# Retention's queries and keys with the head's values on partitions, rope in that layout

## The chip, the cores and the metric

The kernel runs on one core of a Trainium2 chip. The engines of that core are TensorE (PE: matmuls; PEld is its loading of weights, which the profile lists apart), VectorE (DVE), ScalarE (ACT), GpSimd (POOL) and SyncE (SP, which here only issues DMA transfers). On-chip memory has 128 partitions; PE leaves its results in PSUM, in banks of 128 x 512 values.

The metric is device time in microseconds (us), the median over runs. A profiled execution gives the trace from which the rows come. Its span runs from the first to the last instruction.

## The reference

The program is a trunk of two layers over one sequence of 256 tokens with 2048 values each, all in float32. Each layer normalises x, applies a gain and a shift that come from `c` (adaLN), makes one wide projection, feeds three branches (retention, a gated linear recurrence, latent attention), merges them by gates, projects once more and adds the result to x. Retention has 8 heads of 128 values. What bears on the change:

```python
def apply_rope(x, cos, sin):
    half = x.shape[-1] // 2
    x1, x2 = x[..., :half], x[..., half:]
    return concatenate([x1 * cos - x2 * sin, x2 * cos + x1 * sin], axis=-1)

# rope_tables: ang[token, i] = positions[token] * 10000 ** (-2 i / dim), i < dim / 2
cos_ret, sin_ret = rope_tables(positions, 128)     # retention: 64 frequencies
cos_mla, sin_mla = rope_tables(positions, 64)      # latent attention: 32 frequencies

# for each layer
h = rms_norm(x, norm_pre) * (1 + scale) + shift    # scale, shift: from c @ ada_w
rq, rk, rv, rg, lx, lg, mq, mkv, mkr, mg, merge_logits = split(h @ w_in)
q = apply_rope(rq as [256, 8, 128], cos_ret, sin_ret) * 128 ** -0.5
k = apply_rope(rk as [256, 8, 128], cos_ret, sin_ret)
scores = einsum('bnihd,bnjhd->bhnij', q, k) * intra_decay    # and a state between chunks of 64
```

## The kernel before

**Products.** Every weight is split into a head of 12 bits (`wh`, a cast by ACT, L291) and the exact rest (`wl`, a subtraction by DVE, L292), and the activations likewise. A product is then three matmuls, head by head, head by rest, rest by head. Weights come by SP's queue as tiles `raw` of 128 x 2048 values, 1 MB each, in the order in which they are used: one tile is two d-tiles (2 x 128 rows of the weight) by 1024 columns.

Two helpers do the products of 1024 columns over 16 d-tiles. `gemm_x` (matmul on L349) holds the activations still and streams the weights: tokens end on partitions, 128 of them in each half `hf`, and a d-tile takes 12 matmuls of 512 columns. In the last tile of a product the first half of the tokens ends ahead of the second. `gemm_w` (L367 to L369) holds the weights still, in 8 blocks of 128 columns, and streams the 256 tokens: the columns end on partitions, and a d-tile takes 24 matmuls of 256 columns. Both fill four PSUM banks out of six (`acc`); two more (`mi`) are for small work. `group` empties the four, each with one ACT instruction (L396, L398), into two slots of 128 x 1024; where a product of layer 0 is made in parts, DVE adds up the parts (L394). `mode_of` says which helper does which product: `lx`, `lg` and `mg` use `gemm_w`, all others `gemm_x`.

**Order.** The kernel is written as a main run of large products with chains of small work beside them. `tick` is called after each weight tile; it goes through the chains that are ready and lets each do a step. Each engine then runs its own instructions in that order. DMA issues stand on SP's queue (weights, x) and on POOL's (small loads).

In each layer the order is `lx`, `lg`, `mqkv`, `mg`, the gates of `lru`, `mkr`, `rq`, then the two `lru` branch products (`branch`), `rk`, the up-projections of latent attention, `rv`, `rg`, and so on. In the trace, layer 0's `rq` lies around 360 to 408 us, its two `lru` branches at 408 to 455, its `rk` at 506 to 550. In layer 0 the adaLN sums of layer 1 run beside all of that: `ada_sum` lets DVE multiply and add rows of `ada_w` (L452, L454), with a share for ACT (L445) and POOL (L449). In layer 1 no such sums run.

**Retention's queries and keys.** `rq` and `rk` come out of `gemm_x` with tokens on partitions. `ret_chain` waits for `rq`, calls `ret_rope`, which calls `rope` (L592 to L595) four times: two products of 128 x 256 with the sine, one of 128 x 512 with the cosine and one addition of 128 x 512 each, all on DVE. The scores want the head's 128 values on partitions, so `ret_turn` turns the result: four groups for each operand, each of four PE transposes (L771) into one bank `mi`, which ACT copies out (L772), one group for a step of the chain. Then the same for `rk`. Two operands in each of two layers are 16 groups.

**The start.** The first instructions load x, `c`, the vectors and the positions (`pos_i`, L187, on POOL's queue), cast the positions (L189), work out the softplus of `lru_lambda` (from L242 on) and the sums of squares of x (`xtot`, L533), whose square root (L406) gives the norm of x. The rope tables are made later, in the chain `tables`: `k_freq` is loaded onto all partitions (L193, issued at 40.95 us), and 16 operations on DVE make angles, fold them into range and clamp them, each over [128 tokens, 2 halves, 96 frequencies], 64 for retention and 32 for latent attention. Eight ACT instructions take the sines, into `cosr`, `sinr` (retention) and `cosm`, `sinm` (latent attention), all with tokens on partitions.

## Time and profile before

| | before |
|---|---|
| runs, us | 2019.4, 2019.5, 2023.18 |
| median, us | 2019.5 |
| span of the profiled execution, us | 2016.0 |
| instructions in the trace | 25350 |
| DMA, MB moved | 456.98 |
| mean DMA rate over the span, GB/s | 227 |
| granted PE clock, mean over the span (1 is full speed) | 0.991 |

The profiled execution has no time of its own beside its span; the median of the runs is 3.5 us above it, for what lies around the first and the last instruction.

The profile's rows are read like this. An engine's busy time is a sum over instructions. PE's instructions are pipelined, so the duration of one matmul is longer than its share of the time: the distance between starts is what counts. The chain that ended last is followed back from the last instruction to what released each step, and its shares by engine add up to the span. A list of waits says which engine stood idle, for whom, how long in all, how often, and the longest. A timeline has one instruction, or a run of equal ones, in a row: start, duration, engine, line, operation, result and operands, shape; in brackets the idle time ahead of it and what ended it.

### The profile page before, as it was taken

What the parts mean: (1) busy time and instruction counts of PE and PEld (TensorE: products, weight loads), DVE (VectorE), ACT (ScalarE), POOL (GpSimd) and SP (SyncE); (2) the same over time, 40 slices, a digit from 0 to 9 for tenths busy, and PEclk for the clock granted to TensorE, in tenths of its full rate; (3) what the DMA queues carried; (4) which work ended last, traced back from release to release, by engine and by line L of the source; (5) the groups of instructions that cost most, each with busy time, mean ns of one, the idle gap of its engine ahead of it and who ended that gap; (6) DMA issues with size and microseconds to landing.
All of it is one profiled execution on the core that took longest, in us unless ns stands there. A gap on an engine that the chain in (4) does not pass through costs nothing.

```text
span 2016.0 us, 25350 instructions
## 1 busy us (share of the span) xinstructions
PE 1932.3 (96%) x9980; PEld 1624.1 (81%) x9980; DVE 1399.9 (69%) x1812; ACT 991.0 (49%) x1286; POOL 181.6 (9%) x137
## 2 busy tenths in 40 slices
PE   2979999999999999999989999999999999999998
PEld 2867888778988888777879989888898888788886
DVE  7899989787877687767567754446565447786555
ACT  5744538644554544433454774444455444444443
POOL 2242401100000010102010010000000001010100
PEclk9989999999999999999989999999999999999999
DMA  8787863787867777776655555555554557778563
GB/s 294 260 285 272 304 234 120 272 291 245 297 236 252 266 255 259 277 271 217 222 198 189 173 181 188 188 178 181 171 192 147 198 186 250 246 270 282 187 210 125
DMA packets 156936, 456.98 MB, mean 227 GB/s; under 512 B 12144, under 2 KB 20336, under 8 KB 156816
## 3 DMA queue, kind: packets, MB, share of 16 engines
q1 hardware_dynamic: 153248, 443.44, 64.8%
q0 software_dynamic: 3424, 11.65, 1.9%
q8 instruction: 78, 1.28, 0.3%
q14 instruction: 42, 0.34, 0.0%
q10 hardware_dynamic: 144, 0.26, 0.0%
HBM read 451.13 MB, written 4.19 MB: 226 GB/s over the span
## 4 chain that ended last, share of the span: by engine, by line
PE 79%; DVE 11%; DMA 6%; ACT 2%; issue 2%; POOL 0%; SPq 0%; DVEq 0%; ACTq 0%; POOLq 0%
PE acc L349 59%; DMA raw<-in_ada_w 5%; DVE float L454 4%; DVE wl L292 4%; PE acc L368 4%; PE acc L369 4%; PE acc L367 4%; DVE float L394 1%; PE mi L714 1%; PE mi L713 1%; PE mi L871 1%; ACT wh L291 0%; POOL float L891 0%; DMA raw<-in_w_in 0%; PE mi L801 0%
## 5 line engine op out<-in xcount | busy, mean ns | idle before, releaser
L349 PE MATMUL acc<-wh,float32r 128*128 128x512 f32 x4064 | 1159.4, 400 | 4.7 <-DVE float L394 4.4
L292 DVE TENSOR_TENSOR wl<-raw,wh 128x1024 fp32r<-128x1024 f32 (+1 forms) x640 | 794.0, 1244 | 451.9 <-ACT wh L291 445.4
L291 ACT CAST wh<-raw 128x1024 fp32r<-128x1024 f32 (+1 forms) x640 | 666.0, 1042 | 826.0 <-PE acc L349 656.2
L349 PEld LDWEIGHTS acc<-wh,float32r 128*128 128x128 f32 x4064 | 759.2, 189 | 186.3 <-DVE float L394 8.4
L349 PE MATMUL acc<-wl,float32r 128*128 128x512 f32 x2032 | 651.8, 397 | 13.8 <-DVE wl L292 13.8
L349 PEld LDWEIGHTS acc<-wl,float32r 128*128 128x128 f32 x2032 | 381.9, 189 | 110.6 <-DVE wl L292 20.6
L454 DVE SCALAR_TENSOR_TENSOR float<-raw,c_act,float 128x512 f32<-128x512 f32 (+1 forms) x326 | 255.7, 786 | 62.6 <-DMA raw<-in_ada_w 57.9
L367 PE MATMUL acc<-float32r,wh 128*128 128x256 f32 x768 | 218.7, 285 | 5.0 <-ACT float32r L567 5.0
L368 PE MATMUL acc<-float32r,wh 128*128 128x256 f32 x768 | 217.2, 283 | 0.8 <-DVE float32r L568 0.8
L369 PE MATMUL acc<-float32r,wl 128*128 128x256 f32 x768 | 217.1, 283 | 0.7 <-DVE wl L292 0.6
L367 PEld LDWEIGHTS acc<-float32r,wh 128*128 128x128 f32 x768 | 147.2, 192 | 6.3 <-ACT float32r L567 5.8
L368 PEld LDWEIGHTS acc<-float32r,wh 128*128 128x128 f32 x768 | 147.0, 191 | 1.8 <-DVE float32r L568 1.4
L369 PEld LDWEIGHTS acc<-float32r,wl 128*128 128x128 f32 x768 | 146.9, 191 | 1.1 <-DVE wl L292 1.1
L449 POOL TENSOR_TENSOR float<-float,float 128x512 f32<-128x512 f32 (+1 forms) x49 | 70.9, 1448 | 112.5 <-ACT float L445 107.5
L1050 POOL TENSOR_TENSOR float<-float,float 128x512 f32<-128x512 f32 x32 | 52.7, 1663 | 258.5 <-DVE float L1047 243.0
L394 DVE TENSOR_TENSOR float<-acc,float 128x512 f32<-128x512 f32 x96 | 62.5, 682 | 2.8 <-PE acc L349 1.4
L445 ACT ACTIVATE float<-raw,c_act 128x512 f32<-128x512 f32 (+1 forms) x64 | 40.1, 664 | 31.6 <-DMA raw<-in_ada_w 31.5
L793 POOL DMA_DIRECT2D float<-in_ret_gn x4 | 2.3, 570 | 570.0 <-PE mi L739 371.4
L470 PE MATMUL mi<-ident,float 128*128 128x128 f32 x64 | 10.4, 303 | 41.2 <-DVE float L458 41.2
L470 PEld LDWEIGHTS mi<-ident,float 128*128 128x128 f32 x64 | 8.1, 154 | 43.4 <-DVE float L458 42.5
L398 ACT ACTIVATE float<-acc 128x512 f32<-128x512 f32 x56 | 31.7, 598 | 13.0 <-PE acc L349 12.8
L1047 DVE TENSOR_TENSOR float<-acc,float 128x512 f32<-128x512 f32 x48 | 31.8, 683 | 2.4 <-PE acc L349 2.2
(231 smaller groups left out, 1286.2 us busy)
## 6 DMA issues: line engine op xcount, KB each, us to landing
raw<-in_w_in SPq DMA_DIRECT2D x224, 1024.0 KB, 5.1
raw<-in_ada_w SPq DMA_DIRECT2D x96, 1024.0 KB, 6.9
raw<-in_w_branch SPq DMA_DIRECT2D x48, 1024.0 KB, 6.2
raw<-in_w_out SPq DMA_DIRECT2D x32, 1024.0 KB, 5.5
raw<-in_mla_w_ukv SPq DMA_DIRECT2D x8, 1024.0 KB, 6.0
raw<-in_mla_w_uq SPq DMA_DIRECT2D x8, 768.0 KB, 4.5
float<-in_x SPq DMA_DIRECT2D x8, 512.0 KB, 7.5
float<-in_k_decay POOLq DMA_DIRECT2D x4, 512.0 KB, 4.5
```

The costliest lines, as they stand in the source:

```text
L291: nc.scalar.copy(wh, raw[:, c0:c0 + n])
L292: nc.vector.tensor_tensor(out=wl, in0=raw[:, c0:c0 + n], in1=wh.bitcast(F32), op=ALU.subtract)
L349: mm(b[:, 0:w_n], x, ws[:, j * w_n:(j + 1) * w_n], start=st, stop=sp)
L367: mm(dst, wh[:, cs], act.H(kt), start=first, stop=False, skip_group_check=True)
L368: mm(dst, wh[:, cs], act.L(kt), start=False, stop=False, skip_group_check=True)
L369: mm(dst, wl[:, cs], act.H(kt), start=False, stop=last, skip_group_check=True)
L394: nc.vector.tensor_tensor(out=dst, in0=b, in1=dst, op=ALU.add)
L445: nc.scalar.activation(out=t, in_=src, func=AF.Copy, scale=c)
L449: nc.gpsimd.tensor_tensor(out=acc[1], in0=acc[1], in1=t, op=ALU.add)
L454: nc.vector.scalar_tensor_tensor(acc[0], src, c, acc[0], ALU.mult, ALU.add)
L1047: nc.vector.tensor_tensor(out=gate[hf][:, cs], in0=banks[hf][j], in1=gate[hf][:, cs], op=ALU.mult)
L1050: nc.gpsimd.tensor_tensor(out=dst, in0=dst, in1=gate[hf][:, cs], op=ALU.add)
```

## The change

`mode_of` sends `rq` and `rk` to `gemm_w`, so that a result's slot holds, for four heads, the 128 values of a head on partitions and [4 heads, 256 tokens] along the free axis. `ret_rope` works on such a slot: two products with the sine over 64 partitions x 1024, each written to the other half of the partitions, one product of 128 x 1024 with the cosine, and one addition of 128 x 1024. There are two slots for each operand. `ret_turn`, with its transposes and copies, is gone, and the scores read the slots themselves.

For this the tables `cosr` and `sinr` become [128, 256 tokens]: the frequency is a matter of the partition, and the positions stand along the free axis. POOL's queue loads the positions onto all partitions (L191 of the changed kernel), the 64 frequencies as a column, twice (L195), and the 32 frequencies of latent attention as a row onto all partitions (L200). The folding of the angles runs over 256 + 64 = 320 columns in place of 192. The sines of retention take three ACT instructions in place of four; those of latent attention are as before. All other lines of the diff take comments out, and the line numbers move by 6 or so.

```diff
-    NF = HD // 2 + ROPE // 2
-    cosr = cpool.tile([P, 2, HD], F32, name="cosr")
-    sinr = cpool.tile([P, 2, HD], F32, name="sinr")
+    HH, MH = HD // 2, ROPE // 2
+    cosr = cpool.tile([P, T], F32, name="cosr")
+    sinr = cpool.tile([P, T], F32, name="sinr")
...
         nc.vector.tensor_copy(pos, pos_i)
+        row_i = sinr.bitcast(I32)
+        nc.gpsimd.dma_start(out=row_i, in_=a["positions"].partition_broadcast(P))
+        nc.vector.tensor_copy(cosr, row_i)
+        fcol = cpool.tile([P, 1], F32, name="fcol")
+        for i in range(2):
+            nc.gpsimd.dma_start(out=fcol[i * HH:(i + 1) * HH, :], in_=a["k_freq"][:, 0:HH].rearrange("b p -> p b"), allow_slow_non_contiguous=True)
         work = slot()
-        freq = work[:, 0:NF]
-        ang, kk, fold = [work[:, (1 + 2 * i) * NF:(3 + 2 * i) * NF].rearrange("p (a b) -> p a b", b=NF) for i in range(3)]
-        nc.gpsimd.dma_start(out=freq, in_=a["k_freq"].partition_broadcast(P))
+        n = T + ROPE
+        ang, kk, fold = [work[:, i * n:(i + 1) * n] for i in range(3)]
+        freq = work[:, 3 * n:3 * n + MH]
+        nc.gpsimd.dma_start(out=freq, in_=a["k_freq"][:, HH:HH + MH].partition_broadcast(P))
+        nc.vector.tensor_scalar(ang[:, 0:T], cosr, fcol, None, ALU.mult)
         for hf in range(2):
-            nc.vector.tensor_scalar(ang[:, hf, :], freq, pos[:, hf:hf + 1], None, ALU.mult)
+            nc.vector.tensor_scalar(ang[:, T + hf * MH:T + (hf + 1) * MH], freq, pos[:, hf:hf + 1], None, ALU.mult)
         nc.vector.tensor_scalar(kk, ang, 1.0 / TWO_PI, ROUND, ALU.mult, ALU.add)
         nc.vector.tensor_scalar(kk, kk, ROUND, None, ALU.subtract)
...
-        h = HD // 2
-        nc.scalar.activation(out=cosr[:, :, 0:h], in_=kk[:, :, 0:h], func=AF.Sin)
-        nc.scalar.activation(out=cosr[:, :, h:], in_=kk[:, :, 0:h], func=AF.Sin)
-        nc.scalar.activation(out=sinr[:, :, h:], in_=ang[:, :, 0:h], func=AF.Sin)
-        nc.scalar.activation(out=sinr[:, :, 0:h], in_=ang[:, :, 0:h], func=AF.Sin, scale=-1.0)
-        m = ROPE // 2
-        nc.scalar.activation(out=cosm[:, :, 0:m], in_=kk[:, :, h:], func=AF.Sin)
-        nc.scalar.activation(out=cosm[:, :, m:], in_=kk[:, :, h:], func=AF.Sin)
-        nc.scalar.activation(out=sinm[:, :, m:], in_=ang[:, :, h:], func=AF.Sin)
-        nc.scalar.activation(out=sinm[:, :, 0:m], in_=ang[:, :, h:], func=AF.Sin, scale=-1.0)
+        nc.scalar.activation(out=cosr, in_=kk[:, 0:T], func=AF.Sin)
+        nc.scalar.activation(out=sinr[0:HH, :], in_=ang[0:HH, 0:T], func=AF.Sin)
+        nc.scalar.activation(out=sinr[HH:HD, :], in_=ang[HH:HD, 0:T], func=AF.Sin, scale=-1.0)
+        km, am = v3(kk[:, T:n], MH), v3(ang[:, T:n], MH)
+        nc.scalar.activation(out=cosm[:, :, 0:MH], in_=km, func=AF.Sin)
+        nc.scalar.activation(out=cosm[:, :, MH:], in_=km, func=AF.Sin)
+        nc.scalar.activation(out=sinm[:, :, MH:], in_=am, func=AF.Sin)
+        nc.scalar.activation(out=sinm[:, :, 0:MH], in_=am, func=AF.Sin, scale=-1.0)
...
-    def ret_rope(res):
-        for hf in range(2):
-            for j in range(2):
-                cs = slice(j * 512, (j + 1) * 512)
-                rope(res[hf][:, cs], res[hf][:, cs], hf, 4, HD, cosr, sinr)
-
-    def ret_turn(src, tT):
-        for g in range(2):
-            for hf in range(2):
-                b = mbank()
-                for i in range(4):
-                    h = 4 * g + i
-                    nc.tensor.transpose(b[:, i * P:(i + 1) * P], src[hf][:, h * P:(h + 1) * P], ident)
-                nc.scalar.copy(v3(tT[g], T)[:, :, hf * P:(hf + 1) * P], v3(b, P))
-                yield 1
+    def ret_rope(x):
+        t = slot()
+        x3, t3 = v3(x, T), v3(t, T)
+        def table(tb, d0, d1):
+            return tb[d0:d1, :].unsqueeze(1).to_broadcast([d1 - d0, 4, T])
+        for d0, d1 in ((0, HH), (HH, HD)):
+            nc.vector.tensor_tensor(out=t3[HD - d1:HD - d0], in0=x3[d0:d1], in1=table(sinr, d0, d1), op=ALU.mult)
+        nc.vector.tensor_tensor(out=x3, in0=x3, in1=table(cosr, 0, HD), op=ALU.mult)
+        nc.vector.tensor_tensor(out=x, in0=x, in1=t, op=ALU.add)
+        release(t)
     def ret_chain(l, qres, kres, v, gate, act, freed):
-        turned = []
         for src in (qres, kres):
             yield from until(src)
-            ret_rope(src())
-            yield 2
-            t = [slot(), slot()]
-            yield from ret_turn(src(), t)
-            release(*src())
-            turned.append(t)
-        qT, kT = turned
+            for x in src():
+                ret_rope(x)
+                yield 1
+        qT, kT = qres(), kres()
...
         def mode_of(n):
-            return "w" if n in ("lx", "lg", "mg") else "x"
+            return "w" if n in ("lx", "lg", "mg", "rq", "rk") else "x"
```

Where instructions move, the three places that matter are shown as they stand on one engine, before and after. A row has the line, the operation, the result, its operands and its shape; a number behind a name tells buffers apart.

POOL at the start of the program, before (L161 loads the identity, L449 is POOL's share of the adaLN sums):

```order
L161 DMA ident<-in_k_ident 128x128
L187 DMA pos_i<-in_positions 128x2x1
L449 ISA
L449 TENSOR_TENSOR float_7_83<-float_7_83 128x256
L449 TENSOR_TENSOR float_7_83<-float_7_83,float_8_84 128x256
```

and after:

```order
L161 DMA ident<-in_k_ident 128x128
L187 DMA pos_i<-in_positions 128x2x1
L191 DMA sinr<-in_positions 128x256
L195 DMA fcol<-in_k_freq 64x1 x2
L200 DMA float_18_94<-in_k_freq 128x32
L455 ISA
L455 TENSOR_TENSOR float_7_83<-float_7_83 128x256
```

Four loads stand behind `pos_i` and ahead of the adaLN share; the load of `k_freq` further down (L193 of before) is gone.

DVE at the start of the program, before (the cast of the positions, then the softplus, then the sum of squares of x):

```order
L168 MEMSET mmask 64x64
L189 CAST pos<-pos_i 128x2
L242 TENSOR_SCALAR s_386<-e_385 128x8
L243 RECIPROCAL s_386<-s_386 128x8
L244 TENSOR_TENSOR s_386<-s_386,e_385 128x8
L245 TENSOR_TENSOR ss_387<-s_386 128x8
L250 TENSOR_SCALAR e_385<-vec_131 128x8
L246 TENSOR_SCALAR q_388<-ss_387 128x8
L248 SCALAR_TENSOR_TENSOR q_388<-q_388,ss_387 128x8 x6
L249 SCALAR_TENSOR_TENSOR q_388<-q_388,s_386 128x8
L251 SCALAR_TENSOR_TENSOR e_385<-q_388,e_385 128x8
L533 TENSOR_TENSOR xtot_148<-xss_145 128x1
```

and after:

```order
L168 MEMSET mmask 64x64
L189 CAST pos<-pos_i 128x2
L192 CAST cosr<-sinr 128x256
L203 TENSOR_SCALAR float_18_94<-float_18_94,pos 128x32 x2
L248 TENSOR_SCALAR s_386<-e_385 128x8
L249 RECIPROCAL s_386<-s_386 128x8
L250 TENSOR_TENSOR s_386<-s_386,e_385 128x8
L251 TENSOR_TENSOR ss_387<-s_386 128x8
L256 TENSOR_SCALAR e_385<-vec_131 128x8
L252 TENSOR_SCALAR q_388<-ss_387 128x8
L254 SCALAR_TENSOR_TENSOR q_388<-q_388,ss_387 128x8 x6
```

A cast, which reads the loaded positions, and two products, which read the loaded frequencies, have come ahead of the softplus and of the sum of squares.

PE in layer 0, at a border between two weight tiles of an `lru` branch product, before (`mi` is the bank that the transposes fill, `acc` are the banks of the product):

```order
L349 MATMUL acc_3662<-wl_3761,float32r_108 128x512
L349 MATMUL acc_3663<-wl_3761,float32r_108 128x512
L349 MATMUL acc_3662<-wh_3760,float32r_109 128x512
L349 MATMUL acc_3663<-wh_3760,float32r_109 128x512
L771 MATMUL mi_3794<-ident,float_14_90 128x128 x4
L349 MATMUL acc_3660<-wh_3802,float32r_108 128x512
L349 MATMUL acc_3661<-wh_3802,float32r_108 128x512
```

and after:

```order
L355 MATMUL acc_3859<-wl_3950,float32r_108 128x512
L355 MATMUL acc_3860<-wl_3950,float32r_108 128x512
L355 MATMUL acc_3859<-wh_3949,float32r_109 128x512
L355 MATMUL acc_3860<-wh_3949,float32r_109 128x512
L355 MATMUL acc_3857<-wh_3985,float32r_108 128x512
L355 MATMUL acc_3858<-wh_3985,float32r_108 128x512
```

One group of four transposes between the tiles is gone; the tiles' own matmuls follow each other in the same order.

## Rows read from the trace of the kernel before

**Rows 1.** Page: busy time of each engine; the chain's shares by engine.

```profile
PE 1932.3 (96%) x9980; PEld 1624.1 (81%) x9980; DVE 1399.9 (69%) x1812; ACT 991.0 (49%) x1286; POOL 181.6 (9%) x137
...
PE 79%; DVE 11%; DMA 6%; ACT 2%; issue 2%; POOL 0%; SPq 0%; DVEq 0%; ACTq 0%; POOLq 0%
```

**Rows 2.** Stretches: us; busy PE, PEld, DVE, ACT, POOL (instructions); clock; DMA share, GB/s.

```profile
0.00:110.00 110.00, 70.49 (x432) 61.76 (x432) 93.17 (x186) 68.12 (x110) 26.07 (x29) 1.00 0.82 279
408.00:455.00 47.00, 46.53 (x213) 37.58 (x212) 42.82 (x58) 20.81 (x24) 0.00 (x0) 1.00 0.82 277
506.00:550.00 44.00, 44.00 (x324) 41.34 (x324) 39.91 (x60) 26.62 (x40) 0.00 (x0) 1.00 0.85 287
1470.00:1492.00 22.00, 22.00 (x161) 20.64 (x160) 16.97 (x26) 11.89 (x18) 0.00 (x0) 1.00 0.62 190
```

**Rows 3.** Waits of PE, 340 to 980 us: total us, times, longest.

```profile
PE acc L349 <- DVE wl L292: 6.9, 6, 2.4
```

**Rows 4.** Waits of PE, 1040 to 2016 us.

```profile
PE mi L556 <- DVE float L542: 4.9, 1, 4.9
```

**Rows 5.** Chain that ended last, in order of time: start, us, what.

```profile
484.31 22.39 PE acc L349 x96
```

**Rows 6.** Timeline of PE, end of `lg` in layer 1: start, us, instruction.

```profile
1235.76 0.28 PE L369 MATMUL acc<-float32r,wl 128*128 128x256 f32 x1
...
1242.76 0.28 PE L369 MATMUL acc<-float32r,wl 128*128 128x256 f32 x1
1242.87 0.63 PE L349 MATMUL acc<-wh,float32r 128*128 128x512 f32 x2
```

**Rows 7.** Weight loads of L367, kept by shape: ns minimum/median/maximum, first to last start.

```profile
L367 PEld LDWEIGHTS acc<-float32r,wh x768: 186/188/337, 37.7 to 1242.4; 128*128 128x128 f32 x192
```

**Rows 8.** Timeline of PE in layer 0, `rq` and the `lru` branches.

```profile
401.07 0.74 PE L349 MATMUL acc<-wl,float32r 128*128 128x512 f32 x2 [0.92 <-DVE wl L292]
...
429.45 0.60 PE L771 MATMUL mi<-ident,float 128*128 128x128 f32 x4
...
447.53 0.60 PE L771 MATMUL mi<-ident,float 128*128 128x128 f32 x4
```

**Rows 9.** Timeline of DVE in layer 0, rope of `rq` and after.

```profile
412.60 0.42 DVE L592 TENSOR_TENSOR float<-float,sinr 128x256 f32<-128x256 f32 x1
412.94 0.69 DVE L594 TENSOR_TENSOR float<-float,cosr 128x512 f32<-128x512 f32 x1
413.54 0.42 DVE L593 TENSOR_TENSOR float<-float,sinr 128x256 f32<-128x256 f32 x1
...
414.48 2.35 DVE L292 TENSOR_TENSOR wl<-raw,wh 128x1024 fp32r<-128x1024 f32 x2
...
441.03 0.49 DVE L452 TENSOR_SCALAR float<-raw,c_act 128x512 f32<-128x512 f32 x1 [2.09 <-DMA raw<-in_ada_w]
```

**Rows 10.** Timeline of the start, 0 to 32 us.

```profile
1.91 0.72 POOL L187 DMA_DIRECT2D pos_i<-in_positions  x1
...
7.78 0.17 DVE L189 CAST pos<-pos_i 128x2 f32<-128x2 int32 x1 [6.04 <-DMA pos_i<-in_positions]
...
10.39 0.15 DVE L533 TENSOR_TENSOR xtot<-xss 128x1 f32<-128x1 f32 x1
```

**Rows 11.** DMA issues: how many, KB each, median us from issue to landing.

```profile
float<-in_k_freq POOLq DMA_DIRECT2D x1, 48.0 KB, 3.1
pos_i<-in_positions POOLq DMA_DIRECT2D x1, 1.0 KB, 5.8
```

**Rows 12.** Timeline of DVE, 30 to 130 us.

```profile
46.21 0.26 DVE L197 TENSOR_SCALAR float<-float 128x192 f32<-128x192 f32 x1
...
50.70 0.35 DVE L203 TENSOR_TENSOR float<-float 128x192 f32<-128x192 f32 x1
...
68.54 0.49 DVE L452 TENSOR_SCALAR float<-raw,c_act 128x512 f32<-128x512 f32 x1 [2.44 <-DMA raw<-in_ada_w]
...
121.28 0.68 DVE L458 TENSOR_TENSOR float<-float,float 128x512 f32<-128x512 f32 x1
```

## The prediction

> **What bounds the kernel now.** I read the page's first part and its chain of waits first [rows 1]. TensorE (PE) is busy in 96% of a span of 2016.0 us, and 79% of the chain that ended last is PE work; VectorE (DVE) holds 11% of it, DMA 6%. Those two belong mostly to one end of the program: in the first 110 us PE is busy for 70 and DVE for 93 [rows 2], and there the chain runs through DVE, DMA and ScalarE (ACT) while PE waits. From 340 us on the list of what PE waited for is short: 6.9 us in six waits on DVE up to 980 us [rows 3], and 4.9 us once between the layers [rows 4]. So I price the change by two rules: microseconds of PE count in full behind the start, and microseconds of DVE count in full in the start. In between, DVE counts where it is nearly full: in layer 0, beside the adaLN sums, it is busy for 42.8 of 47 us and 39.9 of 44, in layer 1 at the like place for 17.0 of 22 [rows 2].
>
> **The products: the same PE time.** `rq` and `rk` leave `gemm_x` (12 matmuls of 512 columns for each of 16 d-tiles) for `gemm_w` (24 of 256). Busy durations overlap; what counts is the distance between starts. A run of 96 matmuls of `gemm_x` takes 22.39 us, 0.233 us each [rows 5]. The end of `lg` in layer 1, a `gemm_w` product, has 61 matmuls from 1235.76 to 1242.87, 0.117 us each [rows 6]. A d-tile costs 12 x 0.233 = 2.80 us or 24 x 0.117 = 2.80 us: nothing gained, nothing lost. The same weights come in the same order, so DMA, casts and rests stay as they are.
>
> A `gemm_w` product loads weights once per matmul, 188 ns each [rows 7], longer than the 117 ns between its matmuls: the loads lie beside the matmuls. The Trainium skill (TensorE: Matmul & The Clock Gate, Part 3, The mechanism) says that a weight load overlaps running matmuls only where it targets other row groups; that speaks against this change, which doubles the number of full-array loads. This trace disagrees with it, and the rival that would follow is below.
>
> The four result banks now finish 2.1, 1.4, 0.7 and 0 us (6 x 0.117 apart) ahead of a product's end, instead of two by two. The next product has two free banks of six and wants the next ones 6 x 0.233 = 1.4 us after its start, while ACT empties them one by one. The change from `lg` to the product behind it has this very form and shows no gap: 1242.76, then 1242.87 [rows 6]. I cost it at nothing; without that cover it would be a few tenths for each of four products.
>
> **The transposes: 6.9 us off PE.** Sixteen groups of four (L771) go. In layer 0 the first starts at 429.45 and the fourth at 447.53 [rows 8], so 6.03 us lie between two, and one tile of 24 matmuls (24 x 0.233 = 5.60 us) fills all but 0.43 of them. 16 x 0.43 = 6.9 us, half in each layer. Their 16 ACT copies go as well; ACT is busy for 20.8 of 47 us there [rows 2], so that is worth nothing.
>
> **Rope on DVE: from -0.6 to +1.6 us for each operand.** Before, an operand takes eight products of 128x256 and eight operations of 128x512: back to back 0.34 and 0.60 us, 7.5 in all. After, it takes four of 64 partitions x 1024 and four of 128x1024; two of the latter size run in 2.35 us, so 1.14 each with their overlap [rows 9]. No row has 64 partitions: between 0.60 (if half the lanes cost half) and 1.14 the sum is 6.9 to 9.1 us. I take 9.1, since these rows grow with the elements per partition. The Trainium skill (VectorE: DVE Perf Modes, Mode 1x) has one result per lane and cycle, by which idle lanes save nothing; its price, an estimate from its 0.96 GHz, would be 1.07 us, and the sum by it 8.8.
>
> In layer 1 that hides under idle DVE. In layer 0 it does so barely: with four groups (1.7 us) gone and 1.6 us added, the first stretch becomes 44.4 us of DVE in 45.3, the second 41.5 in 42.3 [rows 2]. DVE works in order, and behind a rope operation, or an adaLN sum that waits for its load, stands the rest (`wl`) that PE wants next. A stall of this kind stands at 401 us, 0.92 us [rows 8]. The bounds are -1.0 (such a stall goes, since a `gemm_w` product doesn't hold two tiles to its end) and +3.5 (all of layer 0's gain). On the other side DVE had time to wait 2.09 us for a load ahead of 441 [rows 9]. I take one more stall like that: +0.9.
>
> **The start: +0.9 and +1.4 us.** GpSimd's queue gets four small loads behind `pos_i`, and DVE gets, right behind the cast of `pos_i`, a cast that waits for the positions and two products that wait for the last load, the frequencies. Behind them on DVE stand lambda's softplus and `xtot`, for which ACT's square root waits, and with it the norm of x and all that follows. Before, DVE went on at 7.78 and `xtot` ran at 10.39 [rows 10]. From the wait's end to `xtot`'s end it is 2.8 us, with the new products 2.9: a landing by 8.5 costs nothing, and each microsecond later costs one, since DVE is busy almost without pause behind it [rows 2]. The last load is issued at about 1.91 + 4 x 0.7 = 4.7 us [rows 10]. It lands 3.1 us later if it goes as `k_freq` did, 5.8 if as `pos_i` did (4-byte pieces, in the middle of x) [rows 11]: 7.8 to 10.5. If it starts only when `pos_i` has landed, and takes as long again, it is 13.5. I take 9.4, between the first pair and towards its upper end since it is `pos_i`'s moment: +0.9, bounds 0 and +5.0.
>
> The tables widen from 192 to 320 columns in 16 DVE operations. Between 192 and 512 columns the rows go from 0.26 to 0.49 us with one tensor and from 0.35 to 0.68 with two [rows 12]; 128 columns more are 0.09 and 0.13 us, for nine and seven operations: 1.7. They stand where DVE doesn't pause, but a wait of 2.44 us for a load ends at 68.54, behind them [rows 12]. That load is issued when DVE frees its buffer, so I count most of it: 1.4, bounds 0 and 1.7.
>
> **Sum:** -6.9 + 0.9 + 0.9 + 1.4 = -3.7 us on a span of 2016.0: 2012.3. The three runs have a median of 2019.5, 3.5 above that span, so the time is 2015.8.
>
> **Rivals.**
> - *The start pays nothing and DVE hides its part.* For it: DVE's free time around 441 [rows 9] and a landing as quick as `k_freq`'s [rows 11]. Sum -6.9 to -6.0: 2012.6 to 2013.5. Against: the tables stand where DVE doesn't pause.
> - *Layer 0 becomes bound by DVE.* Its 3.5 us are given back: 2019.5 - 6.9 + 3.5 + 2.3 = 2018.4. For it: 98% in both stretches. Against: PE stalls only briefly where DVE is at 91% [rows 2, 3].
> - *The start waits long (slower).* Four loads in one queue, with 4-byte pieces among megabytes of x and adaLN weights, hold DVE early in its order. The rest of the sum is -4.6, so landing at 13.1 us makes no change, landing at 14.5 gives 2020.9, and only past 17 would it be slower by over 0.2%. Against: `pos_i` itself, twice as many pieces as the new column of frequencies, took 5.8 us [rows 11].
> - *Weight loads show (slower).* If a load couldn't lie beside matmuls, a d-tile would cost 24 x (0.117 + 0.188) = 7.3 us against 12 x (0.233 + 0.188) = 5.1: 64 x 2.2 = 144 us, 2160. `lg`'s rows speak against it [rows 6, 7]. The rule on weight loads named above would do this.
>
> **Chances.** Forecast 0.53, the first rival 0.20, the second 0.14, the third 0.12, the fourth 0.01. A measurement here can tell about 0.2%, 4 us: faster means under 2015.5, slower over 2023.5. Below 2015.5 lie the first rival and a little under half of the forecast: 0.44. Over 2023.5 lie the fourth and a part of the third: 0.05. The rest, 0.51, is no change that can be told. The range takes in the first rival with a stall saved, and at the other end the second and a landing five microseconds late: 2011.8 to 2020.8.
>
> **What would show it.** In the profile after: no L771; `rq` and `rk` at 0.117 us between starts; tiles of the `lru` branches 5.60 us apart; `xtot` later than 10.39 us by as much as the frequencies land late; rope operations of 64 partitions near 1.14 us; few waits of PE on `wl` between 400 and 550 us. I am wrong if `xtot` runs more than 3 us later, if PE's waits in layer 0 grow by more than 3 us, or if a `gemm_w` tile of `rq` takes longer than 5.6 us.

## The result, and the profile after

The changed kernel takes 2005.86 us (four runs, 2000.64 to 2009.57), the kernel before 2021.34 beside it (four runs, 2019.4 to 2023.85): a ratio of 0.9925, interval 0.9904 to 0.9946. Forecast were 2015.8 and a range from 2011.8 to 2020.8. The sign was right, the size was not: 15 us came where 3.7 were expected. The profiled execution has a span of 2002.2 us against 2016.0.

The page of the changed kernel, its first part, answers to [rows 1]:

```profile
PE 1912.2 (96%) x10684; PEld 1668.2 (83%) x10684; DVE 1410.0 (70%) x1782; ACT 984.7 (49%) x1269; POOL 187.9 (9%) x140
```

PE is as full as before, 96%, and its busy time fell from 1932.3 to 1912.2 us, so the 14 us are PE work that takes less time, not waits that went away. The first and the third stretch of [rows 2] in the changed kernel (columns as there):

```profile
0.00:110.00 110.00, 66.91 (x417) 60.36 (x418) 89.93 (x183) 65.70 (x105) 27.69 (x30) 1.00 0.80 271
...
506.00:550.00 44.00, 41.25 (x299) 39.32 (x299) 41.26 (x53) 22.87 (x33) 0.00 (x0) 0.96 0.83 285
```

The start is worse (PE busy for 66.9 us in place of 70.5), and so is the stretch from 506 us on, where PE now stands for 2.75 us. Both losses are in the trace, and the kernel is faster all the same. The gain shows where nothing was changed. Here is a product of `gemm_x` in layer 1 in the chain of the changed kernel (start, us, what), and two matmuls of `mg`, a `gemm_w` product, sixty distances apart in PE's timeline. (The product of [rows 6] is `mg` too, not `lg`: `lg` stands behind `lx` without a gap, and the `gemm_w` product that stands alone between two `gemm_x` products is `mg`. The pace read there holds all the same.)

```profile
1147.93 21.79 PE acc L355 x96
```

```profile
1199.83 0.28 PE L373 MATMUL acc<-float32r,wh 128*128 128x256 f32 x1
...
1207.03 0.28 PE L373 MATMUL acc<-float32r,wh 128*128 128x256 f32 x1
```

96 matmuls of 512 columns took 22.39 us [rows 5] and now take 21.79: 0.227 us each in place of 0.233. Sixty distances of 256 columns took 7.00 [rows 6] and now take 7.20: 0.120 in place of 0.117. One pace became 2.7% faster and the other 2.9% slower, at a granted clock of 1.00 in these stretches of both traces, in products that the diff doesn't touch. So the first question was what sets the pace.

What differs there is an address. The programs place their tiles in on-chip memory in the order of their pools. The changed kernel has one tile more ahead of the weight tiles, the column of frequencies `fcol`: 4 bytes on each partition, which take 32. Byte addresses on a partition, in the two programs as built:

```
                 before    changed
float32r slots   106624    106624     activations: loaded in gemm_x, streamed in gemm_w
wh               195168    195200     weights: streamed in gemm_x, loaded in gemm_w
wl               207456    207488
```

All slots and tiles of a kind are multiples of 256 bytes apart. The distance of weights and activations, modulo 256, was 224 and is now 0. I call it the distance below.

### The profile page after: what moved, and what is told of

It is laid out like the page before. It is cut to its first block, busy times and chain, and to the rows that moved or that the text cites. A ratio compares the mean times of both kernels' runs of the same rounds, so it can differ in the third digit from the quotient of the medians.

```text
span 2002.2 us, 26737 instructions
## 1 busy us (share of the span) xinstructions
PE 1912.2 (96%) x10684; PEld 1668.2 (83%) x10684; DVE 1410.0 (70%) x1782; ACT 984.7 (49%) x1269; POOL 187.9 (9%) x140
## 4 chain that ended last, share of the span: by engine, by line
PE 67%; DVE 17%; DMA 10%; issue 3%; ACT 2%; POOL 0%; DVEq 0%; ACTq 0%; POOLq 0%
PE acc L355 42%; DMA raw<-in_ada_w 9%; DVE float L460 6%; PE acc L374 6%; PE acc L375 6%; PE acc L373 6%; DVE wl L298 6%; DVE float L400 1%; ACT wh L297 1%; DMA raw<-in_w_in 1%; PE mi L719 1%; PE mi L720 1%; DMA float<-in_k_freq 0%; DVE float L774 0%; PE mi L562 0%
## 5 line engine op out<-in xcount | busy, mean ns | idle before, releaser
L355 PE MATMUL acc<-wh,float32r 128*128 128x512 f32 x3552 | 993.1, 394 | 3.9 <-DVE float L400 3.7
L355 PEld LDWEIGHTS acc<-wh,float32r 128*128 128x128 f32 x3552 | 664.5, 189 | 145.2 <-DVE float L400 6.9
L355 PE MATMUL acc<-wl,float32r 128*128 128x512 f32 x1776 | 560.8, 392 | 13.1 <-DVE wl L298 13.1
L355 PEld LDWEIGHTS acc<-wl,float32r 128*128 128x128 f32 x1776 | 333.4, 188 | 89.1 <-DVE wl L298 19.4
L373 PE MATMUL acc<-float32r,wh 128*128 128x256 f32 x1280 | 367.5, 287 | 4.9 <-ACT float32r L573 4.9
L375 PE MATMUL acc<-float32r,wl 128*128 128x256 f32 x1280 | 365.3, 285 | 1.9 <-DVE wl L298 1.9
L374 PE MATMUL acc<-float32r,wh 128*128 128x256 f32 x1280 | 365.1, 285 | 0.8 <-DVE float32r L574 0.8
L373 PEld LDWEIGHTS acc<-float32r,wh 128*128 128x128 f32 x1280 | 248.5, 194 | 6.5 <-ACT float32r L573 5.8
L375 PEld LDWEIGHTS acc<-float32r,wl 128*128 128x128 f32 x1280 | 248.2, 194 | 2.8 <-DVE wl L298 2.7
L374 PEld LDWEIGHTS acc<-float32r,wh 128*128 128x128 f32 x1280 | 248.4, 194 | 1.8 <-DVE float32r L574 1.4
```

The lines of the kernel that those rows point to most:

```text
L355: mm(b[:, 0:w_n], x, ws[:, j * w_n:(j + 1) * w_n], start=st, stop=sp)
L373: mm(dst, wh[:, cs], act.H(kt), start=first, stop=False, skip_group_check=True)
L374: mm(dst, wh[:, cs], act.L(kt), start=False, stop=False, skip_group_check=True)
L375: mm(dst, wl[:, cs], act.H(kt), start=False, stop=last, skip_group_check=True)
```

## Experiments

**The pad alone.** `e1_pad` is the kernel before with an unused tile at the place of `fcol`:

```diff
         nc.vector.tensor_copy(pos, pos_i)
+        pad = cpool.tile([P, 8], F32, name="pad")
+        nc.vector.memset(pad, 0.0)
```

> The kernel before with one unused tile of 32 bytes per partition at the place where the changed kernel has its column of frequencies; nothing else. It moves the weight tiles (raw, wh, wl) up by 32 bytes, from 32 to 0 past a multiple of 64. Theory A, the address of the weight tiles sets the matmuls' pace: matmuls of 512 columns go from 0.233 to 0.227 us apart, those of 256 from 0.117 to 0.120, as between the two profiles at hand; 6096 x -6.7 ns + 2304 x 3.3 ns = -33 us, a span of about 1983 to 1988 (some of it lost to waits on DVE and DMA). Theory B, the pace is that of the chip or of the day: the matmuls' distances are those of the run of before on the same chip, no change in time. Theory C, the pace comes with the changed program (its fewer transposes): no change, 0.233 us, span 2016.

Measured: 2003.01 us (2020.62 before, ratio 0.9913, 0.9894 to 0.9933), span 1996.9. In its chain:

```profile
1144.53 21.79 PE acc L351 x96
```

Theory A holds: 32 unused bytes bring the whole gain, with not a line of the change. Less came than the paces promise (6096 x -6.1 ns + 2304 x 3.1 ns = -30 us; the traces differ by 19). From 362 us on PE waits for `wl` for 15.2 us in place of 9.5, since a quicker PE meets DVE more often; the other 5 us I can't place.

**The change with the bytes moved back.** `e2_after_off` is the changed kernel with 96 more bytes (`[P, 24]` in the pad), which is the place of before modulo 128, but a distance of 96 modulo 256.

> The changed kernel with 96 more unused bytes per partition, so that the weight tiles start at the same place past a multiple of 128 as in the kernel before. Theory A: 0.233 us for 512 columns and 0.117 for 256, and the time goes back to 2014 to 2022 (start +4.8, transposes -7, some waits), no clear gain over before. Theories B and C: 0.227 and 0.120 as in the changed kernel, span about 2002.

Measured: 2022.16 us, 1.0012 of before (1.0002 to 1.0022), span 2019.4; 0.233 us for 512 columns, 0.118 for 256. The gain is gone. That the 256 columns took 0.118 and not 0.117 says that modulo 128 is too coarse.

**Other places.** `e3_pad64` has a pad of 64 bytes, `b128`, `b160` and `b192` have pads of 160, 192 and 224, all in the kernel before. In `e4_act32` a tile of 32 bytes stands ahead of the float32r slots and one of 96 at the pad's place; in `f1_act32_w0` only the first.

```diff
-    store = {dt: [cpool.tile([P, W1], dt, name=f"{dt.name}_{i}") for i in range(n)] for dt, n in NSLOT.items()}
+    store = {F32: [cpool.tile([P, W1], F32, name=f"{F32.name}_{i}") for i in range(NSLOT[F32])]}
+    gap = cpool.tile([P, 8], F32, name="gap")
+    nc.vector.memset(gap, 0.0)
+    store[F32R] = [cpool.tile([P, W1], F32R, name=f"{F32R.name}_{i}") for i in range(NSLOT[F32R])]
```

> The kernel before with 64 unused bytes: the weight tiles move from 96 to 32 past a multiple of 128, the same place past a multiple of 64. Theory A with a period of 64 bytes: no change from before (2016, 0.233 us). If only a multiple of 128 counts, or the sum with something else, the pace differs from 0.233. Theories B and C: no change.

> The kernel before with 32 unused bytes ahead of the float32r slots (the activations move from 0 to 32 past a multiple of 64) and 96 more behind, so that the weight tiles stand as before. In gemm_x the activations are the loaded operand and the weights the streamed one, in gemm_w the other way round. If the streamed operand's address counts alone: gemm_x stays at 0.233 us for 512 columns, gemm_w changes from 0.117 for 256. If the loaded operand's counts too, gemm_x changes.

> The kernel before with 32 unused bytes ahead of the float32r slots: activations at 32, weight tiles at 0 past a multiple of 64, the fourth of the four combinations. Theory A1, only the streamed operand's address counts: gemm_x, which streams weights, as with the 32-byte pad (0.227 us for 512 columns), gemm_w, which streams activations, as with the moved activations (0.114): time about 2303 x 5 ns = 12 us under the 32-byte pad's 2003, so about 1991. Theory A2, only equal places of both operands are bad or good: gemm_x 0.233 or 0.229. Theory A3, both addresses count on their own: gemm_x below 0.227.

> The kernel before with 160 unused bytes: weight tiles 128 past the activations modulo 256. If a distance of a multiple of 64 is what helps: 512 columns in 0.227 to 0.229 us, about 2003. If the distance must be 0 or 64 modulo 256: something else, up to 0.233 and 2020.

> The kernel before with 224 unused bytes: weight tiles 192 past the activations modulo 256. If a distance of a multiple of 64 is what helps: 512 columns in 0.227 to 0.229 us, about 2003. If it goes by 0 and 64 alone: up to 0.233 and 2020.

> The kernel before with 192 unused bytes: weight tiles 160 past the activations modulo 256. If odd multiples of 32 are all alike for gemm_x: 0.233 us for 512 columns, 0.117 to 0.118 for 256, about 2020.

Measured (us from start to start in layer 1, means of about 2,900 matmuls of 512 columns and 1,350 of 256 from PE's timeline, fewer of the first and more of the second in the changed kernels; times of kernels with one run are marked):

| distance | kernels of before | 512 columns | 256 columns | time, us |
|---|---|---|---|---|
| 224 | before | 0.2332 | 0.1168 | 2020.6 |
| 224 | `f1_act32_w0` | 0.2332 | 0.1169 | 2019.9 |
| 0 | `e1_pad` | 0.2271 | 0.1199 | 2003.0 |
| 32 | `e3_pad64` | 0.2333 | 0.1184 | 2026.5 (one run) |
| 64 | `e4_act32` | 0.2290 | 0.1139 | 2002.8 (one run) |
| 128 | `b128` | 0.2324 | 0.1193 | 2018.2 (one run) |
| 160 | `b160` | 0.2342 | 0.1198 | 2028.7 (one run) |
| 192 | `b192` | 0.2333 | 0.1161 | 2020.5 (one run) |

`f1_act32_w0` decides between the readings of an address by itself and a distance: both operands stand 32 bytes further on, and both paces are those of before to 0.1 ns. My A1 (only the streamed operand counts) and A3 are wrong there, and so are two guesses: a multiple of 64 is not what helps (at 128 and 192 it doesn't), and odd multiples of 32 are not alike (at 160 both paces are slower than at 224).

The means of `gemm_w` at 64 and 192 hide two levels. In `e4_act32`, at a granted clock of 1.00 and with the same slots and tiles, sixty distances take 7.07 us in a part of `lx` in layer 0 (the first pair below) and 6.80 in `mg` of layer 1 (the second pair), 0.118 and 0.113 us each:

```profile
207.96 0.28 PE L372 MATMUL acc<-float32r,wh 128*128 128x256 f32 x1
...
215.03 0.28 PE L372 MATMUL acc<-float32r,wh 128*128 128x256 f32 x1
...
1199.82 0.28 PE L374 MATMUL acc<-float32r,wl 128*128 128x256 f32 x1
...
1206.62 0.28 PE L374 MATMUL acc<-float32r,wl 128*128 128x256 f32 x1
```

What puts a run on one level or the other isn't known; at 0 and 224 there is one level, 0.120 and 0.117. Why a distance of 0 or 64 suits `gemm_x`, and not 128, isn't known either. That loading and streaming disturb each other when they read certain places together fits the rows, but nothing here shows it.

The Trainium skill (SBUF — State Buffer, Operand start alignment) says of an operand's start that it must be a multiple of the element's size, that this is about legality and not speed, and that its own runs timed nothing. All distances here are legal, and they are 26 us apart (2002.8 to 2028.7). The Trainium skill (SBUF — State Buffer, SBUF: two separate sides) says that within the engine side only the port pair that GpSimd and VectorE share causes contention; these runs show a pace of PE that goes by where PE's own two operands lie, with the other engines' work the same.

**The change at the distance of before.** `k1_after_same` is the changed kernel with a pad of 224 bytes (`[P, 56]`), so that everything behind it stands 256 bytes further on than in before, at a distance of 224.

> The changed kernel with 224 more unused bytes, so that with its column of 32 the weight tiles stand exactly 256 bytes above those of before: the distance of weight tiles and activations is that of before modulo 256 (224), which the paces so far go by (224: 0.233 and 0.117 us; 0: 0.227 and 0.120; 32 and 96: 0.233 and 0.118; 64: 0.229 and 0.115). This is the change without its side effect. If the pace goes by that distance: 0.233 and 0.117, and 3840 x 1.4 ns = 5.4 us under the 2022.2 of the changed kernel at 96: about 2016.8, against 2020.4 of before. If it doesn't: 0.118 and 2022, slower than before.

Measured: 2018.34 us against 2020.38 (twelve and seventeen runs), 0.9988 (0.9978 to 0.9998), with 0.2332 and 0.1168 us. This is what the change itself does: -2.4 us by the ratio. The prediction had -3.7.

**Where the rest of the forecast went.** PE's waits in the trace of `k1_after_same` between 362 and 715 us (total, times, longest), to be held against [rows 3]:

```profile
PE acc L377 <- DVE wl L300: 4.1, 4, 1.7
PE mi L710 <- DVE adac L479: 3.1, 1, 3.1
```

With two more of 0.2 us they come to 7.6 us. In before the same stretch has 3.1, and no wait of L710's kind:

```profile
PE acc L349 <- DVE wl L292: 2.8, 4, 0.9
PE mi L748 <- DVE adac L471: 0.3, 1, 0.3
```

L710 is the transposes of `mla_rotate` (L702 of before). PE's timeline there:

```profile
544.52 1.04 PE L478 MATMUL mi<-ident,float 128*128 128x128 f32 x8
548.62 0.76 PE L710 MATMUL mi<-ident,float 128*128 128x128 f32 x4 [3.06 <-DVE adac L479]
```

The eight transposes of adaLN (L478) fill both `mi` banks, `mla_rotate` stands right behind them and must wait until DVE, late with adaLN sums and rests, has reduced one bank into `adac`. Before, `ret_turn` took four steps of the chain for each operand, and `mla_rotate` came a weight tile later. The other kernels with the changed chain have this wait too: 2.8 us in the changed kernel itself, 2.4 in `e2_after_off`, 2.6 in `h1_pool`, 2.8 in `a64`. `n1_steps` gives the steps back, empty:

```diff
             for x in src():
                 ret_rope(x)
-                yield 1
+            yield 2
+            for _ in range(4):
+                yield 1
```

> The changed kernel at the address of before (distance 224), with rope's work as one step and then four empty steps of the chain for each operand, as many as the transposes had; this puts mla_rotate's transposes one weight tile behind adaLN's, as before. If the order makes the wait of 2.8 to 3.1 us: it is gone, and the time falls by about 3 us, from 2018.3 to 2015.4. If DVE's load makes it: PE waits as long elsewhere, 2018.

Measured: 2016.40 us against 2021.03, 0.9977 (0.9968 to 0.9985), span 2011.3. The waits of the same stretch:

```profile
PE acc L377 <- DVE wl L300: 1.8, 3, 0.8
PE acc L357 <- DVE wl L300: 1.6, 2, 1.4
PE mi L756 <- DVE adac L479: 0.6, 1, 0.6
```

The wait of L710 is gone, the others come to 4.2 us with one more of 0.2, and they were 4.5: PE does not wait as long elsewhere, so the order made that wait, not DVE's load. This is one trace of each kernel. Against before the kernel is now 4.6 us faster in place of 2.4; the two intervals overlap, so those 2 us are not shown by the times alone.

**The start.** The changed kernel's start (the cast of the positions, the products with the frequencies, `xtot`), which answers to [rows 10]:

```profile
10.59 0.29 DVE L192 CAST cosr<-sinr 128x256 f32<-128x256 int32 x1 [2.73 <-DMA sinr<-in_positions]
...
13.16 0.39 DVE L203 TENSOR_SCALAR float<-float,pos 128x32 f32<-128x32 f32 x2 [2.28 <-DMA float<-in_k_freq]
...
15.99 0.15 DVE L539 TENSOR_TENSOR xtot<-xss 128x1 f32<-128x1 f32 x1
```

The last load landed at about 13.1 us, 8.8 after its issue, and `xtot` ran 5.6 us later than before; PE began at 32.94 in place of 28.16. Two kernels try to give that back. In `g1_late` (and `g2_late_off`, the same with 96 bytes of pad) the cast and the products are queued on DVE behind the first block of h (`h_last` is the last DVE instruction of it); in `h1_pool` GpSimd makes them.

```diff
-        nc.vector.tensor_copy(cosr, row_i)
+        with tc.issue_after(h_last[0]):
+            nc.vector.tensor_copy(cosr, row_i)
...
```

```diff
-        nc.vector.tensor_copy(cosr, row_i)
+        nc.gpsimd.tensor_copy(cosr, row_i)
...
-        nc.vector.tensor_scalar(ang[:, 0:T], cosr, fcol, None, ALU.mult)
+        nc.gpsimd.tensor_scalar(ang[:, 0:T], cosr, fcol, None, ALU.mult)
```

(and the products with `freq` alike).

> The changed kernel as it is (weight tiles at 0 past a multiple of 64) with DVE's cast and products of the tables queued behind the first block of h. First PE instruction at 28.3 us in place of 32.9. If the start's delay counts in full: 4.6 us under the changed kernel's 2005.9, about 2001. If it is given back in waits for weights or adaLN rows: 2004 to 2006.

> The changed kernel with the weight tiles at the place of before (96 past a multiple of 128), and with DVE's cast of the positions and its three products with the frequencies queued behind the first block of h, so that DVE doesn't stand before xtot; loads as in the changed kernel. If the late landing of the frequencies costs what the trace shows (3.8 us at the first PE instruction): first PE instruction at 28.2 us, time 3 to 4 us under the 2022.2 of the changed kernel at this place, about 2018.5, which is 0.1% under before. If the layers give the delay back anyway: no change, 2022.

> The changed kernel as it is, but the cast of the positions and the three products with the frequencies are made by GpSimd, so that DVE's order at the start is that of before. First PE instruction at 28.3 us in place of 32.9. If that delay counts in full: 4.6 us under the changed kernel's 2005.9, about 2001. If PE waits as long later (for the adaLN sums before 130 us): 2004 to 2006.

Measured: `g1_late` 2012.53, 6.7 us slower than the changed kernel; `g2_late_off` 2028.05, 5.9 slower than `e2_after_off`; `h1_pool` 2005.93, the same as the changed kernel, though its PE begins at 30.02. The first PE instruction came at 30.80 us in `g1_late` and at 30.23 in `g2_late_off`, not at 28.3 as expected. In the trace of `g2_late_off` the delay is not gone but moved. The fold of the tables now stands among the adaLN sums before 130 us, and PE waits there, 10.5 us where before waits 6.2:

```profile
126.83 1.11 PE L479 MATMUL mi<-ident,float 128*128 128x128 f32 x4 [10.48 <-DVE float L467]
```

In `h1_pool` the lead of 2.9 us at the first PE instruction has shrunk to 0.3 at the end of `mkr` (365.56 against 365.86 us). In `g2_late_off`, work moved to a later place on DVE cost there. What took back the lead of `h1_pool`, whose DVE has about 1 us less to do, isn't shown: that the beginning is bound by DVE as a whole fits its 91.5 us of work between 30 and 130 us (92.6 in the changed kernel), but is argued only.

**Rope's work on DVE.** `r1_norope` is `g2_late_off` without the call of `ret_rope`.

```diff
             for x in src():
-                ret_rope(x)
                 yield 1
```

> As the kernel with the late tables at the place of before, but without rope's eight DVE operations for each operand (rq and rk go into the scores as they are). Theory: in layer 0 these operations delay the rests and the adaLN sums for which PE waits (2.4 us at 541, 1.9 and 1.1 us at 361 to 432 and around 700), so the time falls by 2 to 4 us to about 2015. Rival: those waits come from the order of the instructions and stay; no change.

Measured: 2034.57, slower than `g2_late_off` by 6.5 us, with less to do. PE's waits between 355 and 730 us came to 9.1 us in place of 5.7. So rope's operations are not what PE waits for; why the time rises without them I didn't find, and both kernels carry the late tables' own loss.

**Each helper at its own distance.** If the pace goes by a product's own operands, both can be had. In `m1_after_split` and `m3_before_split` a weight tile is 256 bytes longer, and `gemm_w` uses it from byte 64 on; the output of ACT's squares, which nobody reads, is made bfloat16 for the room. `m3_before_split` is the kernel before with the pad of `e1_pad`.

```diff
-    def load_split(src, nk, ncol, spare=None):
+    def load_split(src, nk, ncol, spare=None, off=0):
...
-                    wh = whp.tile([P, W1], F32R, tag="wh", name=nm("wh"))[:, 0:n]
+                    wh = whp.tile([P, W1 + 64], F32R, tag="wh", name=nm("wh"))[:, off:off + n]
...
-            for k, (wh, wl) in enumerate(load_split(wsrc(w, r0, k0, nk, c0, W1), nk, W1)):
+            for k, (wh, wl) in enumerate(load_split(wsrc(w, r0, k0, nk, c0, W1), nk, W1, off=16)):
```

> The changed kernel, with weight tiles 256 bytes longer, of which gemm_x uses the first 4096 bytes (distance 0 from the activations, modulo 256) and gemm_w those from byte 64 on (distance 64). The unused output of ACT's squares is bfloat16, which makes the room. If each helper's pace goes by the distance of its own two operands: gemm_x stays at 0.227 us for 512 columns, gemm_w goes from 0.120 to 0.115 for 256, 3840 x 5 ns = 19 us under the changed kernel's 2005.9: about 1987. If the pace belongs to the program's whole layout: both stay, 2006.

> The same in the kernel before with the 32-byte pad: gemm_x at distance 0, gemm_w at 64. By the operands' distance: 2304 x 5 ns = 12 us under the pad's 2003.0: about 1991. Otherwise 2003.

> The changed kernel with activations and weight tiles placed as in the kernel with moved activations (distance 64): 0.229 and 0.115 us. 5328 x 1.7 ns - 3840 x 5.2 ns = -11 us against the changed kernel's 2005.9: about 1995, while the kernel before at this distance took 2002.8: here the change would be worth -8 us, against -2 at 224 and +3 at 0. If the change were worth the same everywhere: about 2001 to 2003.

> The changed kernel with distances 0 for gemm_x and 64 for gemm_w, and the empty steps. By the order theory 3 us under the 1996.2 of the same kernel without them: about 1993, level with the kernel before with both distances (1994.3). By the other 1996.

| kernel | distances | 512, 256 columns | time, us | ratio to before |
|---|---|---|---|---|
| `m1_after_split` | 0 and 64 | 0.2270, 0.1156 | 1996.18 | 0.9871 (0.9853 to 0.9889) |
| `m3_before_split` | 0 and 64 | 0.2271, 0.1167 | 1994.32 | 0.9864 (0.9848 to 0.9879) |
| `n2_split_steps` | 0 and 64 | 0.2270, 0.1155 | 1995.51 | 0.9879 (0.9864 to 0.9894) |
| `a64` | 64 | 0.2290, 0.1138 | 2002.84 | 0.9908 (0.9890 to 0.9926) |

`gemm_x` keeps its pace and `gemm_w` gets faster, so the paces can be set apart. It does not get all of `e4_act32`'s mean at the same distance (0.1139, with the activations 32 bytes further on). Part of its matmuls run on the slower of the two levels named above (in layer 1 of `m1_after_split`, `mg` at 0.1178 and `rq` at 0.1134), and the up-projections of latent attention, for which the tiles are not moved, stay at 0.119 to 0.120. So the distance modulo 256 is not the whole of it for `gemm_w`. `m3_before_split`, the kernel before with addresses moved and the unread squares in bfloat16, beats both kernels: 27 us under the runs of before beside it, and 11.5 under the changed kernel's median, which is from another series of runs. Expected were 1987 and 1991; some of the rest are waits on DVE, as in `e1_pad` (17.7 us for `wl` behind 110 us in `m3_before_split`, 12.3 in before). The empty steps, which took the wait of L710 away at 224, give `n2_split_steps` no difference that these runs can tell (1995.51 against 1996.18): its trace has a like wait of 2.5 us for a bank 100 us later, at attention's output.

`a64` (the changed kernel with the `gap` tile and a pad of 64 bytes) was to gain 8 us over the kernel before at 64 by the paces; it took 2002.84 against 2002.79 in one run. The change is worth about -2 us at 224 (twelve runs), +3 at 0 (2005.86 against `e1_pad`'s 2003.01) and nothing at 64, the last two without an interval of their own.

## Why the prediction was wrong, step by step

- **The products: the step that failed.** I held a d-tile to cost 2.80 us in either helper, and the products that the diff doesn't name to keep their time. The argument holds at the distance of before (`k1_after_same`: 22.40 us for 96 matmuls, 0.1168 us for 256 columns). But I took the pace as given by shape and clock and never asked whether the change moves the operands in memory. With `fcol` ahead of the weight tiles it does: 5328 x -6.1 ns + 3840 x 3.1 ns = -21 us by the paces of layer 1, of which 12.5 arrived between the medians of `k1_after_same` and the changed kernel. At the new distance the two forms are not equal either: a d-tile costs 12 x 0.2271 = 2.73 us in `gemm_x` and 24 x 0.1199 = 2.88 in `gemm_w`, so 64 d-tiles of `rq` and `rk` give 10 us of that away.
- **The transposes: right, as far as layer 1 shows.** Layer 1, from the last matmul of `mkr` to retention's first score, contains eight of the groups and none of DVE's fullness; PE waits in it neither before nor after. It was 339.23 us long and is 335.90 in `k1_after_same`, both in PE's timeline: -3.33, forecast 8 x 0.43 = -3.4. In layer 0 the other half can't be told from the waits there. The first pair is before, the second `k1_after_same`:

```profile
1338.05 0.29 PE L948 MATMUL acc<-float32r,wl 128*64 128x256 f32 x1
...
1677.28 1.03 PE L801 MATMUL mi<-float,float 128*128 128x256 f32 x4
...
1343.04 0.28 PE L950 MATMUL acc<-float32r,wl 128*64 128x256 f32 x1
...
1678.94 0.59 PE L803 MATMUL mi<-float,float 128*128 128x256 f32 x2
```

- **Rope's operations: right in kind, above the upper end in size.** 64 partitions take as long as 128, as I took it. But 1.14 us counted on an overlap of neighbours, and there is none: sixteen operations of 1.220 us are busy for 19.5. Eight come to 9.8 us for an operand, not 9.1, and the 1.07 us estimated for one was too low as well. (The changed kernel's lines of DVE: out<-in, count, busy us, mean ns.)

```profile
L774 DVE TENSOR_TENSOR float<-float,sinr 64x1024 f32<-64x1024 f32 x16 | 19.5, 1220 | 1.1 <-ACT float L402 0.7
L775 DVE TENSOR_TENSOR float<-float,cosr 128x1024 f32<-128x1024 f32 x8 | 9.7, 1218 | 0.0
```

- **Layer 0: mis-sized, and by another mechanism.** Forecast +0.9, bounds -1.0 and +3.5; PE's waits between 362 and 715 us rose by 4.5 us, outside the bounds. 3.1 of them are the wait of `mla_rotate`. It comes a tile earlier because the chain has fewer steps; I priced what the change removes and not what it moves up. The 4.5 us are more than the 3.4 that the transposes were to give in layer 0. That all of layer 0's gain is given back was a rival; it decided there, through one bank and not through DVE's load (`n1_steps`).
- **The start: mis-sized.** I took a landing at 9.4 us and it was 13.1, near the far end of 13.5: the loads behind `pos_i` in POOL's queue took 7.8 to 8.8 us from issue to landing in the changed kernel (9.9 for the last one in `k1_after_same`), not the 3.1 to 5.8 of [rows 11]. The first PE instruction came 4.8 us late in the changed kernel, 6.0 in `k1_after_same`, 3.8 in `n1_steps`; at the end of `mkr` the lag behind before is 4.3 and 3.9 in the last two, against 2.3 forecast with the tables. The tables' rows themselves were well bounded: 0.32 us for 320 columns and 0.48 with two tensors, 0.06 and 0.13 more than 192 columns [rows 12].
- **The sum.** At one distance: forecast -3.7, measured -2.4 (an interval of -4.4 to -0.4). Transposes as forecast, start and layer 0 dearer by some 5 us in the trace; single executions of `k1_after_same` spread over 8 us, so one trace doesn't add up to the medians. By the trace's own terms (-6.9, +4.3, +4.5) the change would cost 2 us, so that -2.4 came near -3.7 does not confirm the terms. The signs named for being wrong all came: `xtot` 5.6 us later, PE's waits in layer 0 up by 4.5 us, and a `gemm_w` tile of `rq` at 48 x 0.1199 = 5.76 us in the changed kernel.
- **The rivals.** Weight loads that show (2160 us) didn't happen: the 1,536 matmuls of 256 columns that `rq` and `rk` now take keep the 0.1168 us of `lx`, `lg` and `mg` at the distance of before. No rival had an address in it, and so none held the measured time.

## What to carry to other kernels

Before a diff is priced, list what it allocates, and where the operands of the costliest loop then stand against each other; a tile of 4 bytes can be worth more than the edit that needs it. An edit is to be compared at equal addresses, with padding put in until they agree. And a chain that loses steps moves all that follows it: price the place that it moves to.

## What the runs showed of the hardware that I had not expected

The distance from start to start of float32r matmuls goes by the place of the two operands against each other: 0.2271 to 0.2342 us for 512 columns and 0.1138 to 0.1199 for 256, at a granted clock of 1.00, in steps of 32 bytes. The same distance gave the same pace in kernels with other work (0: changed kernel, `e1_pad`, `g1_late`, `h1_pool`; 224: before, `f1_act32_w0`, `k1_after_same`, `n1_steps`), and no distance was best for both forms. At 64 the pace for 256 columns is not one number: it was 0.113 or 0.118 us in different products of one trace, so the mean there goes by how many ran on each level. A DVE product over 64 partitions took 1.220 us, one over 128 partitions with as many elements on each 1.218.
